# Transposed blocks by way of HBM, the norm of rows 0 at five boundaries too, and out-projections that end with three units per quarter

## The chip, the core and the metric

The kernel runs on one core of a Trainium2 chip. The metric is device time in microseconds (us) of one execution; less is better. TensorE (PE) multiplies, VectorE (DVE) and ScalarE (ACT) do element work, GpSimd (POOL) does a little of it, SyncE (SP) issues most DMAs. Each engine works through its own fixed list of instructions in order, and a semaphore wait at the head of a list stops all that stands behind it.

## What is computed

A decoder trunk of two layers over 256 rows of 1024 columns. Each layer is a half-step SwiGLU FFN, a mixer (A in layer 0: chunked spatial gating; B in layer 1: causal pooling), and a second half-step FFN, each behind an RMSNorm, and a last RMSNorm:

```
for i in range(DEPTH):
    x = x + 0.5 * swiglu(rmsnorm(x, ffn_norm[i, 0]), ffn_w_in[i, 0], ffn_w_out[i, 0])
    h = rmsnorm(x, mix_norm[i])
    x = x + (chunked_sgu if i % 2 == 0 else pool_mixer)(h, ...)
    x = x + 0.5 * swiglu(rmsnorm(x, ffn_norm[i, 1]), ffn_w_in[i, 1], ffn_w_out[i, 1])
return rmsnorm(x, final_norm)
```

Six sublayers follow each other, so there are five boundaries at which the residual `x` is normed and turned for the next in-projection.

## The kernel before

The 256 rows are two tiles, rows 0 (t = 0) and rows 1 (t = 1), of 128 partitions. Every f32 product is made of three fp32r matmuls (`mm3`, L126 to L131): high by high, high by low, low by high, so each operand is split into a rounded high part (`hh`, `gh`, `whi`) by ACT and the rest (`hl`, `gl`, `wlo`) by DVE.

Weights come in halves of 128x1024 (512 KB). `fetch` issues one on SP's queue into one of four `raw` buffers; `split_piece` makes `whi` on ACT and, two ticks later, `wlo` on DVE, which then issues the next `fetch`. There are eight pairs of split halves (`W_BUFS`): a half can only be split when the half eight before it has been released by PE's last use of it.

The order of all engines' lists is written by the program itself: each `mm3` is one tick, `later(n, fn)` has `fn` recorded n ticks further on, and `pump` records a split every two or three ticks when a buffer is released. So a work item's place in a list is set by ticks (one tick is three matmuls of PE), not by when its data is ready.

`proj_in` computes 512 columns (a chunk) at a time: for rows 0 all eight k, then for rows 1 all eight, with four weight halves; the next four halves serve the next chunk. `proj_out` keeps four accumulators (two rows tiles by two halves of the columns, the quarters). The first `n - LAG` units (256 values of k, two weight halves each) go through all four quarters unit by unit; the last `LAG` units go quarter by quarter, so that each quarter ends on its own: rows 0 left, rows 0 right, rows 1 left, rows 1 right. Behind each quarter stands its residual add (`x<-mm,x`, L361) and `half(t, h)` (L295): multiply by the gain (`xs`, L298), four ticks later four PE transposes of 128x128 into PSUM (`tp<-ident,xs`, L304), then ACT's `hh` and DVE's `hl` from PSUM (L238, L239), then the squares for the norm (L248). The reciprocal root is applied later, behind the in-projection.

The FFN's gated values and mixer A's outputs are needed with k on partitions too. They are turned by DVE in 32x32 squares (`gq<-g`, L374), and 16 DMAs for each pair of chunks move the squares between partition groups from `gq` to `ge`, SBUF to SBUF, half of them issued by SP and half by POOL (L387). `trip` ticks later ACT and DVE split `ge` into `gh` and `gl` (L398, L399): 32 ticks in the FFNs, 24 in mixer A. Mixer B makes its `gh` and `gl` per group from PSUM (L625, L630).

Of the kernel before, what the change touches and what calls it, by code (L numbers as in the profile page):

```python
# [11 lines left out]
F32 = mybir.dt.float32  # L12
F32R = mybir.dt.float32r
AF = mybir.ActivationFunctionType
ALU = mybir.AluOpType

P = 128
# [8 lines left out]
HEADS = 8  # L26
# [4 lines left out]
NCH = FF // 256  # L31
# [4 lines left out]

RAW_BUFS = 4
W_BUFS = 8
LAG = 2
PACE = 3  # L40
LOW = 2
HOP = 3
GATE = 10
T2K = 8
BATCH = 2


@with_exitstack
def trunk_kernel(
# [22 lines left out]
    nc = tc.nc  # L72
    V, A, G, PE = nc.vector, nc.scalar, nc.gpsimd, nc.tensor
# [4 lines left out]
    hp = ctx.enter_context(tc.tile_pool(name="hp", bufs=1))  # L78
    gp = ctx.enter_context(tc.tile_pool(name="gp", bufs=24))
    sq = ctx.enter_context(tc.tile_pool(name="sq", bufs=2))  # L80
    tmp = ctx.enter_context(tc.tile_pool(name="tmp", bufs=2))
    tiny = ctx.enter_context(tc.tile_pool(name="tiny", bufs=4))
    pm = ctx.enter_context(tc.tile_pool(name="pm", bufs=6, space=bass.MemoryType.PSUM))
# [8 lines left out]
    def f32(ap):  # L92
        return ap.bitcast(F32)

    def t2k(name):
        return tmp.tile([P, 512], F32, name=name, tag="t2k", bufs=T2K)

    def g_tile(name, cols=None):
        return gp.tile(cols or [P, 2, S], F32R, name=name, tag="g2k")
# [6 lines left out]
    def later(n, fn):  # L106
        pending.append([n, fn])
# [28 lines left out]
    for i in range(DEPTH):  # L136
        j = i // 2
# [93 lines left out]
    def scaled(a, b, name):  # L231

        o = tiny.tile([P, 1], F32, name=name, tag="scaled", bufs=12)
        V.tensor_scalar(o, a, b, None, op0=ALU.mult)
        return o

    def split(ps, hi, lo, gap=1):
        A.copy(hi, ps)  # L238
        low = lambda: V.tensor_tensor(lo, ps, f32(hi), op=ALU.subtract)  # L239
        if gap:  # L240
            later(gap, low)
        else:
            low()

    def square(t, c):
        sq = t2k("sq")
        a = tiny.tile([P, 1], F32, name="ssq", bufs=6)
        A.activation(sq[:, :c.stop - c.start], x[t][:, c], AF.Square, scale=1.0 / 32.0, accum_out=a)  # L248
        return a

    def rstd(t, parts):
        ms = tiny.tile([P, 1], F32, name="ms")
        V.tensor_scalar(ms, parts[0], parts[1], EPS, op0=ALU.add, op1=ALU.add)  # L253
        return rsqrt(ms, f"rstd{t}")

    def norm_T(gain, factors):


        hT = [[None, None, None, []] for _ in range(NT)]
        ssq = {0: [], 1: []}  # L260

        def tiles(t, h):
            if h == 0:
                for e, n in enumerate(("hh", "hl")):
                    hT[t][e] = hp.tile([P, KD * P], F32R, name=f"{n}{t}", tag=f"{n}{t}")
            return hT[t][:2]

        def stat(t, h):
            ssq[t].append(square(t, slice(h * 512, (h + 1) * 512)))
            if h == 1:  # L270
                later(1, lambda: rows(t))

        def rows(t):
            r = hT[t][2] = rstd(t, ssq[t])
            later(1, lambda: hT[t][3].extend(scaled(r, r if f is None else f, f"r{t}") for f in factors))

        def first(t, h):

            ps = pt.tile([P, 4, P], F32, name="tp", tag="tp")
            for e in range(4):  # L280
                k = 4 * h + e
                PE.transpose(ps[:, e, :], x[t][:, k * P:(k + 1) * P], ident)  # L282
            c = slice(h * 512, (h + 1) * 512)
            hh, hl = tiles(t, h)
            xs = t2k("xs")
            g = gcol[:, 4 * h:4 * h + 4].unsqueeze(2).to_broadcast([P, 4, P])
            V.tensor_tensor(xs.rearrange("p (k t) -> p k t", k=4), ps, g, op=ALU.mult)

            def fin():
                A.copy(hh[:, c], xs)  # L290
                V.tensor_tensor(hl[:, c], xs, f32(hh[:, c]), op=ALU.subtract)  # L291

            return fin

        def half(t, h):  # L295
            c = slice(h * 512, (h + 1) * 512)
            xs = t2k("xs")
            V.tensor_tensor(xs, x[t][:, c], gain[0][:, c], op=ALU.mult)  # L298
            state["hush"] = 4

            def turn():
                ps = pt.tile([P, 512], F32, name="tp", tag="tp")
                for k in range(4):
                    PE.transpose(ps[:, k * P:(k + 1) * P], xs[:, k * P:(k + 1) * P], ident)  # L304
                hh, hl = tiles(t, h)
                split(ps, hh[:, c], hl[:, c])
                later(2, lambda: stat(t, h))

            later(4, turn)

        return half, first, stat, hT

    def proj_in(chunks, hT, use, first=False):
# [20 lines left out]
    def proj_out(n, lhs, scale, half, tail=False):  # L334
# [7 lines left out]
        def part(u, t, h):  # L342
            c = segs[t][h]
            for j in range(2):
                k = 2 * u + j
                if len(w) <= k:
                    w.append(take())
                hi, lo = w[k]
                mm3(acc[t][h], *lhs(k, t), hi[:, c], lo[:, c], k == 0, k == 2 * n - 1)
                if t == NT - 1 and c.stop == D:  # L350
                    release()

        for u in range(n - LAG):
            for t in range(NT):
                for h in range(len(segs[t])):
                    part(u, t, h)
        for t in range(NT):
            for h, c in enumerate(segs[t]):
                for u in range(n - LAG, n):
                    part(u, t, h)  # L360
                V.scalar_tensor_tensor(x[t][:, c], acc[t][h], scale(t), x[t][:, c], op0=ALU.mult, op1=ALU.add)  # L361
                half(t, h)

    def turned(n, out, trip, closing=False):

        squares = {}

        def put(c, t, src):  # L370
            b, m = c // BATCH, min(BATCH, n - c // BATCH * BATCH)
            if b not in squares:
                squares[b] = sq.tile([P, 4, m, 2, NT, 32], F32, name="gq", tag="gq")
            V.transpose(  # L374
                squares[b][:, :, c % BATCH, :, t, :].rearrange("p q k i -> p k q i"),
                src.rearrange("p (k q j) -> p k q j", k=2, q=4),
            )
            if t == NT - 1 and c % BATCH == m - 1:
                later(2, lambda: move(b, m))

        def move(b, m):

            e = sq.tile([P, 4, m, 2, NT, 32], F32, name="ge", tag="ge")
            to = "p c k t i -> p (c k t i)"
            for q in range(4):
                for a in range(4):
                    (G if a % 2 else nc.sync).dma_start(e[32 * q:32 * q + 32, a].rearrange(to), squares[b][32 * a:32 * a + 32, q].rearrange(to))  # L387
            if closing and b == (n - 1) // BATCH:
                G.drain()
            for c in range(m):  # L390
                later(trip + 3 * c, lambda c=c: take_in(b * BATCH + c, e[:, :, c]))

        def take_in(c, e):
            hi, lo = g_tile("gh"), g_tile("gl")
            src = e.rearrange("p a k t i -> p a (k t) i")
            to = "p k (t a i) -> p a (k t) i"
            h, l = (x.rearrange(to, t=NT, a=4) for x in (hi, lo))
            A.copy(h, src)  # L398
            later(1, lambda: V.tensor_tensor(l, src, f32(h), op=ALU.subtract))  # L399
            out[c] = hi, lo  # L400

        return put

    def ffn(i, hT, half, first=False, tail=False):

        gT, rh, r2 = {}, {}, {}
        put = turned(NCH, gT, 32, closing=tail)

        def use(c, t, ps):
            if c == 0:  # L410
                rh[t], r2[t] = hT[t][3]
            th = tmp.tile([P, 256], F32, name="th", tag="c1k", bufs=2)
            A.activation(th, ps[:, 0:256], AF.Tanh, scale=rh[t])  # L413

            def mul():
                s = tmp.tile([P, 256], F32, name="s", tag="c1k", bufs=2)
                V.scalar_tensor_tensor(s, th, 1.0, ps[:, 0:256], op0=ALU.add, op1=ALU.mult)  # L417
                g = tmp.tile([P, 256], F32, name="g", tag="g1k", bufs=4)
                V.scalar_tensor_tensor(g, s, r2[t], ps[:, 256:512], op0=ALU.mult, op1=ALU.mult)  # L419
                later(1, lambda: put(c, t, g))  # L420

            later(1, mul)

        proj_in(NCH, hT, use, first)

        def lhs(k, t):
            hi, lo = gT[k // 2]
            return hi[:, k % 2, t * P:(t + 1) * P], lo[:, k % 2, t * P:(t + 1) * P]

        proj_out(NCH, lhs, lambda t: 0.25, half, tail)  # L430
# [13 lines left out]
    def mixer_a(j, hT, half, prep, next_gain):  # L444
        vn_g, wm, bs = prep
        vn_g.append(load_gain(a_v_norm[j, D:2 * D]))
        r, vs, ssq, yT, ws, k_sq, k_th, half_r, rv = {}, {}, {0: [], 1: []}, {}, {}, {}, {}, {}, {}
# [83 lines left out]
                    later(GATE + t_, lambda t_=t_: gate(q, t_))  # L531

        us = {}
        put = turned(HEADS, yT, 24)

        def gate(q, t):
            vh, vl = vs[q, t]
# [138 lines left out]
    with tc.manual_schedule(engines={E.PE, E.Activation, E.DVE, E.Pool, E.SP}):  # L676
# [28 lines left out]
        _, first, stat, hT = norm_T(None, FFN_R)  # L705
# [106 lines left out]
```

## Time and profile before

| what | value |
| --- | --- |
| median of 3 runs | 937.83 us (937.55 to 939.37) |
| the profiled execution, own time | 938.44 us |
| its span in the trace | 936.7 us |
| PE busy | 927.7 us (99%), granted clock 0.998 |
| DVE, ACT, POOL busy | 649.2, 478.1, 135.3 us |
| DMA | 195.63 MB, mean 209 GB/s |

The span is what the instructions cover; the execution's own time is 1.7 us longer. Busy time of PE includes matmuls that overlap (one takes 390 ns and the next starts some 227 ns later), so what counts on PE is the distance from start to start and any gap in it.

### The profile page before, as it was taken

The numbers are of one execution on the slowest core, as the hardware profiler recorded it, in microseconds if no ns is written. First come the engines' busy times: TensorE is split into PE (matmuls) and PEld (weight loads), VectorE is DVE, ScalarE is ACT, GpSimd is POOL, SyncE is SP. The second block draws the span as 40 slices with busy tenths as digits, with TensorE's granted clock in tenths as the row PEclk, the third lists the DMA queues.
The fourth block names the chain that finished last, engine by engine and source line by source line (L and its number), as shares of the span: only waits on it lengthen the run. The fifth ranks groups of instructions, "written<-read, shape, count | busy, mean of one in ns | idle before, by whom it ended". The sixth has DMA issues, their size and how long they took to land.

```text
span 936.7 us, 12478 instructions
## 1 busy us (share of the span) xinstructions
PE 927.7 (99%) x4238; PEld 769.4 (82%) x4238; DVE 649.2 (69%) x880; ACT 478.1 (51%) x641; POOL 135.3 (14%) x256
## 2 busy tenths in 40 slices
PE   9999999999999999999999999999999999999997
PEld 6888888888888888888888888888888888888886
DVE  6877774578898686777645867775467787777642
ACT  6555554368765364554533545545355464445431
POOL 0111130013233001112200032111000002221100
PEclk9999999999999999999999999999999999999999
DMA  6777877556477647776754677777555566677731
GB/s 239 234 246 253 240 260 234 177 193 198 149 241 238 212 164 222 223 241 212 241 193 135 225 218 223 230 242 254 185 173 183 180 205 222 211 246 212 232 123 45
DMA packets 68960, 195.63 MB, mean 209 GB/s; under 512 B 13216, under 2 KB 20896, under 8 KB 68896
## 3 DMA queue, kind: packets, MB, share of 16 engines
q1 hardware_dynamic: 61152, 187.22, 62.0%
q0 software_dynamic: 7168, 6.83, 2.6%
q10 hardware_dynamic: 576, 0.79, 0.2%
q8 instruction: 33, 0.54, 0.2%
q14 instruction: 31, 0.25, 0.1%
HBM read 180.11 MB, written 1.05 MB: 193 GB/s over the span
## 4 chain that ended last, share of the span: by engine, by line
PE 98%; DVE 1%; DMA 0%; ACT 0%; issue 0%; POOLq 0%; POOL 0%; ACTq 0%
PE mm L128 32%; PE mm L129 32%; PE mm L130 32%; PE tp L304 1%; DMA x<-in_x 0%; PE tp L129 0%; PE tp L130 0%; PE tp L128 0%; PE mm L697 0%; DVE x L361 0%; PE tp L282 0%; ACT sq L248 0%; PE tp L603 0%; PE tp L604 0%; PE tp L606 0%
## 5 line engine op out<-in xcount | busy, mean ns | idle before, releaser
L180 DVE TENSOR_TENSOR wlo<-raw,whi 128x1024 fp32r<-128x1024 f32 (+1 forms) x334 | 401.6, 1215 | 157.0 <-ACT whi L175 148.2
L175 ACT CAST whi<-raw 128x1024 fp32r<-128x1024 f32 (+1 forms) x334 | 343.4, 1042 | 221.0 <-PE mm L130 150.9
L128 PE MATMUL mm<-whi,hh 128*128 128x512 f32 x864 | 338.3, 392 | 0.1
L129 PE MATMUL mm<-wlo,hh 128*128 128x512 f32 x864 | 336.4, 389 | 0.0
L130 PE MATMUL mm<-whi,hl 128*128 128x512 f32 x864 | 336.4, 389 | 0.0
L130 PEld LDWEIGHTS mm<-whi,hl 128*128 128x128 f32 x864 | 162.3, 188 | 34.4 <-DVE hl L291 0.4
L128 PEld LDWEIGHTS mm<-whi,hh 128*128 128x128 f32 x864 | 162.4, 188 | 33.9 <-ACT hh L290 0.5
L129 PEld LDWEIGHTS mm<-wlo,hh 128*128 128x128 f32 x864 | 162.4, 188 | 32.9
L128 PE MATMUL mm<-whi,gh 128*128 128x512 f32 (+1 forms) x470 | 179.4, 382 | 0.0
L130 PE MATMUL mm<-whi,gl 128*128 128x512 f32 (+1 forms) x470 | 178.4, 379 | 0.0
L129 PE MATMUL mm<-wlo,gh 128*128 128x512 f32 (+1 forms) x470 | 178.3, 379 | 0.0
L387 POOL DMA_DIRECT2D ge<-gq x224 | 110.3, 500 | 400.1 <-ACT gh L398 245.7
L413 ACT ACTIVATE th<-mm,r 128x256 f32<-128x256 f32 x88 | 41.8, 475 | 129.6 <-PE mm L130 128.3
L130 PEld LDWEIGHTS mm<-whi,gl 128*128 128x128 f32 x470 | 88.4, 188 | 16.9
L129 PEld LDWEIGHTS mm<-wlo,gh 128*128 128x128 f32 x470 | 88.5, 188 | 16.2
L128 PEld LDWEIGHTS mm<-whi,gh 128*128 128x128 f32 x470 | 88.4, 188 | 16.2
L417 DVE SCALAR_TENSOR_TENSOR s<-th,mm 128x256 f32<-128x256 f32 x88 | 37.1, 421 | 61.1 <-ACT th L413 61.0
L228 POOL TENSOR_TENSOR rstd<-ms,neg_half 128x1 f32<-128x1 f32 x14 | 7.8, 554 | 344.2 <-DVE ms L253 344.2
L419 DVE SCALAR_TENSOR_TENSOR g<-s,r,mm 128x256 f32<-128x256 f32 x88 | 42.3, 481 | 3.1
L374 DVE STREAM_TRANSPOSE gq<-g 128x256 f32<-128x256 f32 x88 | 39.2, 445 | 2.9
L238 ACT CAST hh<-tp 128x512 fp32r<-128x512 f32 x20 | 11.8, 589 | 47.6 <-PE tp L304 47.6
L399 DVE TENSOR_TENSOR gl<-ge,gh 128x512 fp32r<-128x512 f32 x52 | 35.3, 684 | 0.0
(86 smaller groups left out, 337.7 us busy)
## 6 DMA issues: line engine op xcount, KB each, us to landing
raw<-in_ffn_w_in SPq DMA_DIRECT2D x174, 512.0 KB, 4.6
raw<-in_ffn_w_out SPq DMA_DIRECT2D x88, 512.0 KB, 5.0
raw<-in_a_w_in SPq DMA_DIRECT2D x32, 512.0 KB, 4.1
raw<-in_a_w_out SPq DMA_DIRECT2D x16, 512.0 KB, 5.0
ge<-gq POOLq DMA_DIRECT2D x192, 32.0 KB, 4.4
ge<-gq SPq DMA_DIRECT2D x192, 32.0 KB, 4.1
raw<-in_b_w_in SPq DMA_DIRECT2D x8, 512.0 KB, 3.8
raw<-in_b_w_out SPq DMA_DIRECT2D x8, 512.0 KB, 4.7
```

Of the source, the lines that this page charges most:

```text
L128: PE.matmul(acc, lhsT=ah, rhs=bh, start=start, stop=False)
L129: PE.matmul(acc, lhsT=ah, rhs=bl, start=False, stop=False)
L130: PE.matmul(acc, lhsT=al, rhs=bh, start=False, stop=stop)
L175: A.copy(hi[:, c], raw[:, c])
L180: V.tensor_tensor(lo[:, c], raw[:, c], f32(hi[:, c]), op=ALU.subtract)
L238: A.copy(hi, ps)
L374: V.transpose(squares[b][:, :, c % BATCH, :, t, :].rearrange("p q k i -> p k q i"), src.rearrange("p (k q j) -> p k q j", k=2, q=4),)
L387: (G if a % 2 else nc.sync).dma_start(e[32 * q:32 * q + 32, a].rearrange(to), squares[b][32 * a:32 * a + 32, q].rearrange(to))
L399: later(1, lambda: V.tensor_tensor(l, src, f32(h), op=ALU.subtract))
L413: A.activation(th, ps[:, 0:256], AF.Tanh, scale=rh[t])
L417: V.scalar_tensor_tensor(s, th, 1.0, ps[:, 0:256], op0=ALU.add, op1=ALU.mult)
L419: V.scalar_tensor_tensor(g, s, r2[t], ps[:, 256:512], op0=ALU.mult, op1=ALU.mult)
```

## The change

1. A new DRAM pool `hbm` (two buffers). `quadrants` writes all squares of a batch from `gq` to HBM in one DMA, and `TURN` = 4 ticks later issues four DMAs that read them back into the four partition groups of `ge`. All five are on SP's queue. `turned` uses it in place of the 16 DMAs; POOL issues no DMA any more, and the drain of POOL in the last FFN is gone.
2. At the boundaries `half` for rows 0 no longer uses PE: DVE turns `xs` in 32x32 squares at once, `quadrants` moves them by way of HBM, and `WAY` = 11 ticks later ACT and DVE split `ge` into `hh` and `hl`. Rows 1 keep the PE transposes.
3. `LAG` goes from 2 to 3: the last three units are done quarter by quarter, 18 matmuls in each quarter where there were 12.
4. Mixer A's `trip` goes from 24 to 17 ticks.

```diff
-LAG = 2
+LAG = 3
+TURN = 4
+WAY = 11
+    hbm = ctx.enter_context(tc.tile_pool(name="hbm", bufs=2, space=bass.MemoryType.DRAM))
...
-            later(4, turn)
+            def across():
+                z = sq.tile([P, 4, 4, 32], F32, name="gq", tag="gq")
+                V.transpose(z.rearrange("p q k i -> p k q i"), xs.rearrange("p (k q j) -> p k q j", k=4, q=4))
+                e = sq.tile([P, 4, 4, 32], F32, name="ge", tag="ge")
+                quadrants(z.rearrange("p q k i -> p q (k i)"), [e[32 * q:32 * q + 32].rearrange("p a k i -> p a (k i)") for q in range(4)], P)
+                later(WAY, lambda: take_in(e))
+            def take_in(e):
+                hh, hl = (o[:, c].rearrange("p (k a i) -> p a k i", k=4, a=4) for o in tiles(t, h))
+                A.copy(hh, e)
+                later(1, lambda: V.tensor_tensor(hl, e, f32(hh), op=ALU.subtract))
+                later(2, lambda: stat(t, h))
+            if t == 0:
+                across()
+            else:
+                later(4, turn)
...
+    def quadrants(squares, to, n):
+        d = hbm.tile([P, 4, n], F32, name="dq", tag="dq")
+        nc.sync.dma_start(d, squares)
+        src = d.rearrange("(a j) q n -> q j a n", a=4)
+        def back():
+            for q in range(4):
+                nc.sync.dma_start(to[q], src[q])
+        later(TURN, back)
...
-            for q in range(4):
-                for a in range(4):
-                    (G if a % 2 else nc.sync).dma_start(e[32 * q:32 * q + 32, a].rearrange(to), squares[b][32 * a:32 * a + 32, q].rearrange(to))
-            if closing and b == (n - 1) // BATCH:
-                G.drain()
+            quadrants(squares[b].rearrange("p q c k t i -> p q (c k t i)"), [e[32 * q:32 * q + 32].rearrange("p a c k t i -> p a (c k t i)") for q in range(4)], m * 128)
...
-        put = turned(HEADS, yT, 24)
+        put = turned(HEADS, yT, 17)
```

In the rows below the numbers behind the names are buffers; line numbers of the changed kernel are its own (L178 there is L175 before, L183 is L180, L241 is L238, L251 is L248, L381 is L361, L301 is L298, L307 is L304, L131 to L133 are L128 to L130).

First place: ACT's list at the first boundary, from the FFN to mixer A. Before:

```order
L175 CAST whi_1698<-raw_1636 128x1024
L175 CAST whi_1713<-raw_1651 128x1024
L238 CAST hh0_1742<-tp_1737 128x512
L248 ACTIVATE sq_1755,ssq_1756<-x0_85 128x512
L238 CAST hh0_1742<-tp_1764 128x512
L248 ACTIVATE sq_1780,ssq_1781<-x0_85 128x512
L238 CAST hh1_1798<-tp_1793 128x512
L175 CAST whi_1807<-raw_1672 128x1024
L248 ACTIVATE sq_1824,ssq_1825<-x1_86 128x512
L238 CAST hh1_1798<-tp_1836 128x512
L175 CAST whi_1842<-raw_1687 128x1024
```

And in the changed kernel:

```order
L178 CAST whi_1604<-raw_1542 128x1024
L178 CAST whi_1619<-raw_1557 128x1024
L322 CAST hh0_1691<-ge_1639 128x4x4x32
L251 ACTIVATE sq_1704,ssq_1705<-x0_87 128x512
L241 CAST hh1_1721<-tp_1716 128x512
L178 CAST whi_1724<-raw_1578 128x1024
L322 CAST hh0_1691<-ge_1669 128x4x4x32
L251 ACTIVATE sq_1735,ssq_1736<-x1_88 128x512
L251 ACTIVATE sq_1752,ssq_1753<-x0_87 128x512
L241 CAST hh1_1721<-tp_1774 128x512
L178 CAST whi_1780<-raw_1593 128x1024
```

Before, the four halves of the next in-projection's first chunk (1662, 1677, 1698, 1713) are split ahead of the boundary and 1807 is already of the second chunk; in the changed kernel only two (1604, 1619) are, and the third (1724) and fourth (1780) stand behind the two casts of `hh1`, which wait for the transposes of rows 1. DVE's list there, in the changed kernel:

```order
L381 SCALAR_TENSOR_TENSOR x0_87<-mm_1289,x0_87 128x512
L301 TENSOR_TENSOR xs_1665<-x0_87,gain_938 128x512
L315 STREAM_TRANSPOSE gq_1667<-xs_1665 128x4x4x32
L323 TENSOR_TENSOR hl0_1692<-ge_1639,hh0_1691 128x4x4x32
L381 SCALAR_TENSOR_TENSOR x1_88<-mm_1290,x1_88 128x512
L301 TENSOR_TENSOR xs_1699<-x1_88,gain_938 128x512
L242 TENSOR_TENSOR hl1_1722<-tp_1716,hh1_1721 128x512
L183 TENSOR_TENSOR wlo_1725<-raw_1578,whi_1724 128x1024
L323 TENSOR_TENSOR hl0_1692<-ge_1669,hh0_1691 128x4x4x32
L381 SCALAR_TENSOR_TENSOR x1_88<-mm_1291,x1_88 128x512
L301 TENSOR_TENSOR xs_1743<-x1_88,gain_938 128x512
```

The residual add and the gain of the last quarter (`x1<-mm_1291`, `xs_1743`) now stand behind `wlo_1725` and both `hl0`; before, they stood behind the `hl0` of the second transposes and some operations of one column.

Second place: PE's list at the same boundary in the changed kernel, from the second turn of rows 1 on (`mm_1747` is rows 0 of the first chunk):

```order
L307 MATMUL tp_1774<-ident_89,xs_1743 128x128 x4
L131 MATMUL mm_1747<-whi_1724,hh0_1691 128x512
L132 MATMUL mm_1747<-wlo_1725,hh0_1691 128x512
L133 MATMUL mm_1747<-whi_1724,hl0_1692 128x512
L131 MATMUL mm_1747<-whi_1724,hh0_1691 128x512
L132 MATMUL mm_1747<-wlo_1725,hh0_1691 128x512
L133 MATMUL mm_1747<-whi_1724,hl0_1692 128x512
L131 MATMUL mm_1747<-whi_1780,hh0_1691 128x512
L132 MATMUL mm_1747<-wlo_1781,hh0_1691 128x512
```

Eighteen matmuls stand between the two turns of rows 1, as before; between the second turn and the first use of the fourth half (`whi_1780`, `wlo_1781`) stand six. The other four boundaries have the same rows in the same places.

Third place: PE's list in mixer B of the changed kernel, behind the last group's matmuls (`tp_6565`, split into `gh_6578`, `gl_6579`):

```order
L133 MATMUL tp_6565<-qh_6510,wlo_6241 128x256
L131 MATMUL mm_6461<-whi_6469,gh_6550 128x512
L132 MATMUL mm_6461<-wlo_6470,gh_6550 128x512
L133 MATMUL mm_6461<-whi_6469,gl_6551 128x512
L131 MATMUL mm_6461<-whi_6513,gh_6550 128x512
L132 MATMUL mm_6461<-wlo_6514,gh_6550 128x512
L133 MATMUL mm_6461<-whi_6513,gl_6551 128x512
L131 MATMUL mm_6461<-whi_6531,gh_6578 128x512
L132 MATMUL mm_6461<-wlo_6532,gh_6578 128x512
L133 MATMUL mm_6461<-whi_6531,gl_6579 128x512
L131 MATMUL mm_6461<-whi_6582,gh_6578 128x512
L132 MATMUL mm_6461<-wlo_6583,gh_6578 128x512
```

Before, 18 matmuls of the second unit stood between the last group and the first quarter's two last units; now the last group's own values are used six matmuls behind it, and `whi_6582` and `wlo_6583` stand behind its `gh` on ACT and its `gl` on DVE.

## Rows read from the trace of the kernel before

**Rows 1.** The page: busy time by engine, and the last chain by engine.

```profile
PE 927.7 (99%) x4238; PEld 769.4 (82%) x4238; DVE 649.2 (69%) x880; ACT 478.1 (51%) x641; POOL 135.3 (14%) x256
...
PE 98%; DVE 1%; DMA 0%; ACT 0%; issue 0%; POOLq 0%; POOL 0%; ACTq 0%
```

**Rows 2.** Waits of PE: us in total, times, longest.

```profile
PE mm L697 <- DVE warm L692: 1.3, 1, 1.3
PE tp L282 <- DMA x<-in_x: 1.0, 2, 0.8
```

**Rows 3.** Timeline of PE, first boundary, second turn of rows 1: start, us.

```profile
195.23 0.60 PE L304 MATMUL tp<-ident,xs 128*128 128x128 f32 x4
195.58 0.48 PE L128 MATMUL mm<-whi,hh 128*128 128x512 f32 x1
195.89 0.40 PE L129 MATMUL mm<-wlo,hh 128*128 128x512 f32 x1
196.13 0.40 PE L130 MATMUL mm<-whi,hl 128*128 128x512 f32 x1
...
197.05 0.40 PE L128 MATMUL mm<-whi,hh 128*128 128x512 f32 x1
197.29 0.39 PE L129 MATMUL mm<-wlo,hh 128*128 128x512 f32 x1
```

**Rows 4.** Timeline of ACT at the first boundary.

```profile
195.86 0.59 ACT L238 CAST hh<-tp 128x512 fp32r<-128x512 f32 x1 [1.02 <-PE tp L304]
196.34 1.05 ACT L175 CAST whi<-raw 128x1024 fp32r<-128x1024 f32 x1
```

**Rows 5.** Timeline of DVE at the first boundary.

```profile
183.12 0.69 DVE L361 SCALAR_TENSOR_TENSOR x<-mm,x 128x512 f32<-128x512 f32 x1 [1.08 <-PE mm L130]
183.84 0.69 DVE L298 TENSOR_TENSOR xs<-x,gain 128x512 f32<-128x512 f32 x1
...
185.85 0.69 DVE L361 SCALAR_TENSOR_TENSOR x<-mm,x 128x512 f32<-128x512 f32 x1 [0.17 <-PE mm L130]
...
190.37 0.68 DVE L239 TENSOR_TENSOR hl<-tp,hh 128x512 fp32r<-128x512 f32 x1
190.97 0.20 DVE L253 TENSOR_SCALAR ms<-ssq 128x1 f32<-128x1 f32 x1
...
197.43 1.22 DVE L180 TENSOR_TENSOR wlo<-raw,whi 128x1024 fp32r<-128x1024 f32 x1 [0.26 <-ACT whi L175]
...
199.63 1.22 DVE L180 TENSOR_TENSOR wlo<-raw,whi 128x1024 fp32r<-128x1024 f32 x1
200.77 0.68 DVE L455 SCALAR_TENSOR_TENSOR ga<-ga,mm 128x512 f32<-128x512 f32 x1
```

**Rows 6.** DMA issues: operation, count, KB each, median us to landing.

```profile
raw<-in_a_w_in SPq DMA_DIRECT2D x32, 512.0 KB, 4.1
...
ge<-gq SPq DMA_DIRECT2D x192, 32.0 KB, 4.1
...
out<-o SPq DMA_DIRECT2D x2, 256.0 KB, 2.0
```

**Rows 7.** Lines L374 and L387: ns min/median/max; landing us min/median/max.

```profile
L374 DVE STREAM_TRANSPOSE gq<-g x88: 436/446/449, 23.4 to 870.6; 128x256 f32<-128x256 f32 x88
...
L387 SPq DMA_DIRECT2D ge<-gq x224: 507/589/1693, 39.2 to 877.5; - x112
...
DMA to landing us min/median/max: 1.7/4.3/6.4
```

**Rows 8.** Timeline of mixer B behind its last group: PE, ACT, DVE.

```profile
732.35 0.40 PE L128 MATMUL mm<-whi,gh 128*128 128x512 f32 x1
...
732.55 0.84 ACT L625 ACTIVATE gh<-tp,sc 128x256 fp32r<-128x256 f32 x2 [1.98 <-PE tp L130]
...
733.43 0.88 DVE L630 SCALAR_TENSOR_TENSOR gl<-tp,sc,gh 128x256 fp32r<-128x256 f32 x2 [1.94 <-ACT gh L625]
734.37 1.23 DVE L180 TENSOR_TENSOR wlo<-raw,whi 128x1024 fp32r<-128x1024 f32 x1
```

**Rows 9.** PE's warm-up, and windows: us, busy by engine, granted clock.

```profile
1.26 2.31 PE L697 MATMUL mm<-warm 128*128 128x512 bf16 x5 [1.26 <-DVE warm L692]
...
930.00:937.00 7.00, 0.00 (x0) 0.00 (x0) 1.47 (x6) 1.51 (x6) 0.55 (x1) 0.65 0.20 75
```

More of the change, by code (lines that the diff above doesn't have):

```diff
@@ L362, in proj_out, with turned @@
                 half(t, h)
-    def turned(n, out, trip, closing=False):
+    def quadrants(squares, to, n):
[6 more added lines that the diff above has]
+        later(TURN, back)
+    def turned(n, out, trip):
         squares = {}
@@ L383, in move @@
             e = sq.tile([P, 4, m, 2, NT, 32], F32, name="ge", tag="ge")
-            to = "p c k t i -> p (c k t i)"
-            for q in range(4):
-                for a in range(4):
-                    (G if a % 2 else nc.sync).dma_start(e[32 * q:32 * q + 32, a].rearrange(to), squares[b][32 * a:32 * a + 32, q].rearrange(to))
-            if closing and b == (n - 1) // BATCH:
-                G.drain()
+            quadrants(squares[b].rearrange("p q c k t i -> p q (c k t i)"), [e[32 * q:32 * q + 32].rearrange("p a c k t i -> p a (c k t i)") for q in range(4)], m * 128)
             for c in range(m):
@@ L406, in ffn @@
         gT, rh, r2 = {}, {}, {}
-        put = turned(NCH, gT, 32, closing=tail)
+        put = turned(NCH, gT, 32)
         def use(c, t, ps):
```

## The prediction

> **What bounds the kernel now.** The page comes first: PE is busy for 99% of the span, and the chain that ended last runs through PE for 98% [rows 1]. The list of PE's waits then tells whether that is work or waiting: it has two entries, both at the start, 2.3 us in all [rows 2]. So past its first microseconds PE never waits for anyone, and the time is the sum of the distances between its matmuls. Only two things can move it: fewer instructions on PE, or a wait where there is none. For a wait the views of one boundary matter, engine by engine [rows 3 to 5], since every engine's order is fixed ahead.
>
> I count time at a boundary from the first matmul behind the first quarter (rows 0 left). The residual add of a quarter starts 0.2 behind that point. Two adds in a row without a turn between them stand 2.73 apart (183.12 and 185.85, [rows 5]) for 12 matmuls, so a matmul is 0.227 and a new quarter of 18 is 4.09.
>
> **What is removed.** Forty PE transposes, ten groups of four. A group starts at 195.23 and the second matmul behind it at 195.89: 0.66 where two starts are otherwise 0.23 apart, so a group costs 0.43 to 0.45; with 0.44, ten groups are **4.4 us less** [rows 3]. Nothing else leaves PE.
>
> **What the longer quarters do to the weights (LAG).** There are eight pairs of split halves. With two units held for four quarters four are held and four free, which are the first chunk's four halves. With three units six are held, so halves 3 and 4 of the next chunk can only be split in and behind the last quarter. The order shows where: on ACT each stands behind a cast of `hh1`, which waits for a PE transpose of rows 1.
>
> *The fourth half.* Before, the same chain can be read behind the second turn: transposes at 195.23, cast 195.86, `whi` 196.34, `wlo` 197.43 to 198.65, that is 3.42 from start to end [rows 3 to 5]. Nobody waited for that half, since it belonged to the second chunk. Now PE wants it behind six matmuls: the row that takes `wlo` is the eighth behind the turn, which stood at 197.29, 2.06 behind the start. 3.42 + 0.05 for the semaphore - 2.06 = **1.4 us per boundary, 7.0 for five**.
>
> *The third half.* On DVE its `wlo` and then an `hl0` stand ahead of the last quarter's add and gain, which the second turn needs. From the start of the first turn: cast 0.63 later, `whi` 0.48 later, `wlo` 1.09 later, then 1.14 to the next operation (199.63 to 200.77), `hl0` 0.60 (190.37 to 190.97), add 0.72 (183.12 to 183.84), gain 0.69, semaphore 0.05: 5.40 [rows 3 to 5]. PE reaches the second turn after 0.44 + 18 x 0.227 = 4.53. It waits **0.87 per boundary, 4.4 for five**. What is queued behind it on PE is the whole in-projection. The fourth half starts from that turn, so the two waits add.
>
> **What the way through HBM does.** For rows 0 left: add at 0.2, gain 0.72 later, DVE transposes 0.72 later. A transpose of 128x256 takes 0.446 [rows 7], so one of 512 columns between that and 0.89; I take 0.7. SP issues the write at 2.4. The nearest row for a write to HBM of the same 256 KB is the output at the end, on an idle queue: 2.0 [rows 6]. At 4.4 the four reads are issued, at some 0.6 each [rows 7], the last at 6.2. Their landing no row shows. The nearest by shape is the move of squares, 1.7 at best and 4.3 in the median, with weight loads in flight [rows 7]. The order has no weight load between the write and the reads here, so I take 2.0, like the output: 8.2 to 8.3. Then cast, `hl0`, add, gain of rows 1 left (0.65 + 0.65 + 0.72 + 0.69 and semaphores, 2.76): its turn can start at 11.0, where PE arrives at 2 x 4.09 + 12 x 0.227 = 10.9. So 0.1 at the low end, zero with a landing of 1.7, and 2.4 with 4.3. The last weight load was issued 3 us before the write and takes 4.1 in the median [rows 6], so the write may land some tenths later: I take **0.4 for each of four boundaries, 1.6**. For rows 0 right the same steps start at 4.3, but SP is busy with the first reads until 6.7: landing at 12.3 to 12.5, where the third half's chain asks for it at 13.5. That one is covered by 1 us. At the fifth boundary (mixer B to FFN) the order has a weight load between the first write and its reads and one ahead of the second write; at up to 4.1 each I add 0.4 more to the first and 0.9 to the second, **1.7 there**. Together 3.3 (bounds 0 and 13).
>
> The Trainium skill, "DMA: Bandwidth & Descriptors", section "Anatomy of one DMA", puts a fixed cost of about 2.0 us on each DMA, most of it the confirmed write at the target, heaviest at HBM. By it (an estimate from that page) each trip pays this twice in a row; the output's 2.0 agrees, the squares' 4.3 is more than that page gives for 32 KB within SBUF, and with 4.3 for the reads the total below would be 9 us higher.
>
> **Mixer B.** The last group's matmuls end as 732.35 starts. `gh` is done 1.04 behind that point, `gl` 1.96, `whi` of the last half 1.98, its `wlo` at 735.60, 3.25 [rows 8]. Now PE wants `gl` at 8 x 0.23 = 1.85 and that `wlo` at 10 x 0.23 + 0.15 of waiting, 2.5: waits of 0.15 and 0.8, **0.95 once**.
>
> **At nothing.** The pairs of chunks: 2.0 to 4.1 for the write, 2.4 for four issues, 2.0 to 4.3 for the last read, 6 to 11, against 32 ticks of 0.68 (21.8) in the FFNs. In mixer A 17 ticks are 11.6, and the last pair is wanted about 6 ticks (4.1) later still; two weight loads stand between its write and reads, which would use up that cover but not exceed it. Five DMAs on SP replace eight on SP and eight on POOL; SP now stops until the write lands, and the weight loads behind it come up to 4 later; eight split halves are 8 x 2.72 of PE's time. POOL loses its issues and the drain, and nobody waits for POOL there. The end is unchanged: the last add hangs on PE's last matmul either way.
>
> **Sum.** -4.4 + 7.0 + 4.4 + 3.3 + 0.95 = +11.2. On the profiled execution's own 938.44 that is 949.7; it stands 0.6 above the median of the runs, so I forecast **949.1 us**, 1.2% slower.
>
> **The rivals.**
> - *The transposes saved are all that counts: 933.4 us.* This ends on the other side. It needs both halves' splits to be done in time: the two waits decide, and the change breaks even where they fall from 2.27 to 0.88 per boundary (with nothing for the trip). For it: no chain of ACT and DVE ever held PE up before [rows 2], and steps between two rows may hold idle time that shrinks. Against it: in the chains read above ACT and DVE start each step as soon as its input is there or the step ahead of it lets them, and the halves' places in the lists are fixed.
> - *Only one of the two waits appears.* If `hl0` and the add of the last quarter get ahead of the third half's `wlo` in effect, 4.4 goes and 944.7 remains; with the trip at its lower bound of 0 too, 941.4.
> - *The reads land like the squares, 4.3 us.* Then the first turn waits 2.4 at four boundaries and about 3.7 at the fifth: 13.3 in place of 3.3, 959.1 us. For it: the median of 224 moves [rows 7]; against: no weight load is issued into that gap.
> - *The clock falls in the new waits.* The granted clock is at its full level of 2.4 GHz throughout and falls only where PE has been idle at the end [rows 9]. The warm-up matmuls took 2.31 for five, 0.46 each, twice the 0.227. If 24 matmuls behind each boundary ran like that, 24 x 0.23 x 5 = 28 us more, 977. Pauses of 0.8 at the start [rows 2] changed nothing. [...]
>
> **How the numbers follow.** The forecast's case has 0.61, one wait only 0.12, late reads 0.13, the clock 0.03, the bare saving 0.07, and 0.04 for a balance of waits and saving. A measurement of this kernel tells 0.2% from no change, here 1.9 us. Faster is the bare saving and a little of the balance, 0.08; within 0.2% 0.03; slower 0.89. The range of 941 to 957 holds the forecast with its trip between 0 and about 11, and the case of one wait; what it leaves out is the bare saving, the latest reads and the clock.
>
> **What would show each step.** In the changed kernel's list of PE's waits: about 1.4 us five times at a high-by-low matmul, released by DVE's `wlo`; about 0.9 five times at the transposes, released by DVE's `xs`; a few tenths at the first turn, released the same way, with ACT's `hh` waiting for `ge`; two short waits in mixer B. The write `dq<-gq` at the boundaries should land in 2 to 3 us and the reads in about 2. PE should have 40 transposes left. I am wrong if PE's waits stay under 4 us in all (then the saving wins), if ACT's wait for `ge` exceeds 3 us at each boundary, or if the granted clock shows its lower level in the middle of the span.

## The result, and the profile after

The changed kernel takes **950.33 us** (median of 4 runs, 949.76 to 952.73); the kernel before, beside it, 937.90 (4 runs). The ratio is 1.0134, with a 95% interval of 1.0122 to 1.0146: 1.3% slower. The profiled execution took 950.13 us, with a span of 948.3, 11.6 more than the span before.

The page after, busy time and last chain by engine, answers to [rows 1].

```profile
PE 927.6 (98%) x4198; PEld 764.3 (81%) x4198; DVE 655.3 (69%) x890; ACT 475.3 (50%) x641; POOL 25.6 (3%) x32
...
PE 82%; DVE 8%; DMA 5%; ACT 2%; issue 2%; SPq 0%; POOL 0%; ACTq 0%; POOLq 0%; DVEq 0%
```

PE has 40 instructions fewer and hardly less busy time: a matmul counts as busy for its modelled 0.39, while in a row the next starts after 0.227, so some 0.16 of every gap is counted as busy, and that hides much of what the transposes saved. The chain says what happened: it no longer stays on PE, but leaves it for DVE, DMA and ACT, which hold 15% of the span together. The list of PE's waits after names the places (it answers to [rows 2]):

```profile
PE tp L307 <- DVE xs L301: 6.0, 6, 1.6
PE mm L132 <- DVE wlo L183: 4.9, 7, 0.8
PE mm L723 <- DVE warm L718: 1.3, 1, 1.3
PE mm L131 <- ACT whi L178: 1.2, 5, 0.2
PE tp L285 <- DMA x<-in_x: 1.1, 2, 0.7
```

Two of the five are the old ones of the start. The other three are new, 12.1 us in 18 waits. A wait in this list begins only at that modelled end, so the gaps below are measured from start to start, less the normal distance. The timeline of PE at the first boundary, second turn of rows 1 (it answers to [rows 3]):

```profile
193.97 0.39 PE L133 MATMUL mm<-whi,hl 128*128 128x512 f32 x1
195.06 0.66 PE L307 MATMUL tp<-ident,xs 128*128 128x128 f32 x4 [0.71 <-DVE xs L301]
...
196.71 0.39 PE L133 MATMUL mm<-whi,hl 128*128 128x512 f32 x1
197.34 0.51 PE L131 MATMUL mm<-whi,hh 128*128 128x512 f32 x1 [0.24 <-ACT whi L178]
198.60 0.51 PE L132 MATMUL mm<-wlo,hh 128*128 128x512 f32 x1 [0.76 <-DVE wlo L183]
```

Before the turn 1.09 from start to start, so 0.86 lost; then 0.63 and 1.26, so 0.40 and 1.03 lost on the fourth half. Between the two turns of rows 1 stand 18 matmuls here; in the kernel before there were 12 (turns at 192.04 and 195.23), and not 18 as the section on the change has it. The lists of ACT and DVE there show what the turn and that half waited for (they answer to [rows 4, 5]). ACT:

```profile
190.77 1.05 ACT L178 CAST whi<-raw 128x1024 fp32r<-128x1024 f32 x1
...
195.76 0.59 ACT L241 CAST hh<-tp 128x512 fp32r<-128x512 f32 x1 [2.18 <-PE tp L307]
196.24 1.05 ACT L178 CAST whi<-raw 128x1024 fp32r<-128x1024 f32 x1
```

DVE:

```profile
191.86 1.22 DVE L183 TENSOR_TENSOR wlo<-raw,whi 128x1024 fp32r<-128x1024 f32 x1 [0.26 <-ACT whi L178]
193.00 0.68 DVE L323 TENSOR_TENSOR hl<-ge,hh 128x512 fp32r<-128x512 f32 x1
193.60 0.68 DVE L381 SCALAR_TENSOR_TENSOR x<-mm,x 128x512 f32<-128x512 f32 x1
194.32 0.69 DVE L301 TENSOR_TENSOR xs<-x,gain 128x512 f32<-128x512 f32 x1
...
197.32 1.23 DVE L183 TENSOR_TENSOR wlo<-raw,whi 128x1024 fp32r<-128x1024 f32 x1 [0.25 <-ACT whi L178]
```

From 190.77 on there is no pause in the chain `whi`, `wlo`, `hl0`, add, gain, turn. ACT's cast of the fourth half (196.24) stands behind a cast that needs the turn (195.76), and ACT idles 2.18 in front of that cast. SP's queue at the first and at the second boundary shows the way through HBM:

```profile
181.16 0.33 SPq L387 DMA_DIRECT2D dq<-gq  x1
183.18 1.75 SPq L392 DMA_DIRECT2D ge<-dq  x4
...
318.21 1.47 SPq L165 DMA_DIRECT2D raw<-in_ffn_w_in  x2
321.48 0.33 SPq L387 DMA_DIRECT2D dq<-gq  x1
325.19 1.75 SPq L392 DMA_DIRECT2D ge<-dq  x4
```

The reads are issued when the write has landed: 2.0 later at the first boundary; 3.7 later at the second, where two weight loads of 512 KB were issued just ahead, 3.3 and 2.1 before the write. At the first the last load was issued 3.5 before it. Medians of all writes and reads of these sizes, ten of the boundaries and four of the FFNs' last chunks (DMA issues, to [rows 6]):

```profile
dq<-gq SPq DMA_DIRECT2D x14, 256.0 KB, 2.2
ge<-dq SPq DMA_DIRECT2D x56, 64.0 KB, 2.0
```

All gaps that are new, boundary by boundary:

| place | gaps, us | sum | forecast |
| --- | --- | --- | --- |
| second turn of rows 1 (third half) | 0.86, 0.94, 0.84, 0.89, 1.60 | 5.13 | 4.4, and 0.9 of the trip at the fifth |
| fourth half, `whi` and `wlo` | 1.43 five times | 7.15 | 7.0 |
| first turn of rows 1 (trip) | 0, 1.80, 0, 0, 0.26 | 2.06 | 2.4 |
| mixer B, out-projection | 0.99 | 0.99 | 0.95 |
| mixer B, in-projection | 0.48 | 0.48 | none |
| transposes that went | | -4.4 | -4.4 |

That is 15.8 less 4.4, 11.4 of the 11.6 by which the span grew.

### The profile page after: what moved, and what is told of

Read it like the earlier page. It is cut to its first block, busy times and chain, and to the rows that moved or that the text cites. A ratio compares the mean times of both kernels' runs of the same rounds, so it can differ in the third digit from the quotient of the medians.

```text
span 948.3 us, 11685 instructions
## 1 busy us (share of the span) xinstructions
PE 927.6 (98%) x4198; PEld 764.3 (81%) x4198; DVE 655.3 (69%) x890; ACT 475.3 (50%) x641; POOL 25.6 (3%) x32
## 4 chain that ended last, share of the span: by engine, by line
PE 82%; DVE 8%; DMA 5%; ACT 2%; issue 2%; SPq 0%; POOL 0%; ACTq 0%; POOLq 0%; DVEq 0%
PE mm L132 27%; PE mm L133 27%; PE mm L131 26%; DVE wlo L183 3%; DMA dq<-gq 2%; ACT whi L178 2%; DMA raw<-in_a_w_out 1%; DMA ge<-dq 1%; DVE xs L301 1%; DVE x L381 1%; DVE y L574 1%; SPq L392 0%; DMA x<-in_x 0%; DVE hl L323 0%; DVE u L489 0%
## 5 line engine op out<-in xcount | busy, mean ns | idle before, releaser
L183 DVE TENSOR_TENSOR wlo<-raw,whi 128x1024 fp32r<-128x1024 f32 (+1 forms) x334 | 399.9, 1213 | 141.5 <-ACT whi L178 136.6
L178 ACT CAST whi<-raw 128x1024 fp32r<-128x1024 f32 (+1 forms) x334 | 341.4, 1039 | 204.9 <-PE mm L133 130.3
L131 PE MATMUL mm<-whi,hh 128*128 128x512 f32 x864 | 338.3, 392 | 1.2 <-ACT whi L178 1.2
L133 PE MATMUL mm<-whi,hl 128*128 128x512 f32 x864 | 336.3, 389 | 0.0
L131 PEld LDWEIGHTS mm<-whi,hh 128*128 128x128 f32 x864 | 162.4, 188 | 36.8 <-ACT whi L178 3.3
L133 PEld LDWEIGHTS mm<-whi,hl 128*128 128x128 f32 x864 | 162.2, 188 | 34.2 <-DVE hl L294 0.4
L131 PE MATMUL mm<-whi,gh 128*128 128x512 f32 (+1 forms) x470 | 178.9, 381 | 0.0
L133 PE MATMUL mm<-whi,gl 128*128 128x512 f32 (+1 forms) x470 | 178.2, 379 | 0.0
L133 PEld LDWEIGHTS mm<-whi,gl 128*128 128x128 f32 x470 | 88.4, 188 | 16.7
L131 PEld LDWEIGHTS mm<-whi,gh 128*128 128x128 f32 x470 | 88.4, 188 | 16.5 <-ACT whi L178 0.2
L424 ACT CAST gh<-ge 128x512 fp32r<-128x512 f32 x52 | 31.8, 618 | 4.9 <-DMA ge<-dq 4.9
L322 ACT CAST hh<-ge 128x512 fp32r<-128x512 f32 x10 | 6.2, 620 | 51.9 <-DMA ge<-dq 51.9
L381 DVE SCALAR_TENSOR_TENSOR x<-mm,x 128x512 f32<-128x512 f32 (+1 forms) x21 | 13.9, 663 | 22.1 <-PE mm L133 22.1
```

Of the source, the lines that this page charges most:

```text
L131: PE.matmul(acc, lhsT=ah, rhs=bh, start=start, stop=False)
L133: PE.matmul(acc, lhsT=al, rhs=bh, start=False, stop=stop)
L178: A.copy(hi[:, c], raw[:, c])
L183: V.tensor_tensor(lo[:, c], raw[:, c], f32(hi[:, c]), op=ALU.subtract)
```

## The experiments

The theory (**held halves**): three units per quarter hold six of eight pairs, so the third and fourth half of the next chunk are split behind the casts of the turns; that is what makes PE wait. The rival (**trip**): the norm's way through HBM makes the boundary late, and the waits on weights only show it.

**The parts, one at a time.** First the kernel before with only the longer quarters and mixer A's 17 ticks; nothing goes through HBM.

```diff
-LAG = 2
+LAG = 3
-        put = turned(HEADS, yT, 24)
+        put = turned(HEADS, yT, 17)
```

> The kernel before with LAG = 3 and mixer A's trip of 17 ticks, and nothing else: all turns on PE, squares moved within SBUF. Theory W (the weight halves that six held buffers push behind the casts of hh1 hold PE up): the fourth half costs 1.4 us at each of five boundaries as in the changed kernel, the third half only about 0.3 each, since no hl0 stands ahead of the last quarter's add here (5.40 - 0.60 against 4.53), and mixer B 1.0: 937.9 + 7.0 + 1.4 + 1.0 = 947.3 us. Rival T (the trip through HBM, on which ACT waits 52 us in the changed kernel, is what costs): there is no trip, so about 938, plus at most 1 for mixer B.

949.59 us (949.50 to 949.88), ratio 1.0123 [1.0108, 1.0138]. Without any trip, and without the transposes' saving, it is 11.5 slower, 2.3 more than the theory had. Its gaps: 1.43 at each of the five fourth halves, 0.33 to 0.39 at each second turn of rows 1, 1.00 and 0.47 in mixer B, 0.24 at the second turn of rows 0 at the fifth boundary, 10.6 of the 11.1 by which the span (947.8) is longer. The list of PE's waits of this kernel:

```profile
PE mm L129 <- DVE wlo L180: 4.9, 7, 0.8
...
PE mm L128 <- ACT whi L175: 1.2, 5, 0.2
PE tp L304 <- DVE xs L298: 1.0, 5, 0.2
```

The waits on `wlo` and `whi` are the same, to a tenth, as in the changed kernel (4.9 and 1.2). At the second turn of rows 1 the gap is only 0.33 to 0.39; `hl0` (0.60) does not stand in DVE's list there. So the changed kernel is made up of this one's 11.5, some 0.5 for `hl0` at each of five boundaries and 2.8 of late trips, less 4.4 for the transposes. That gives 12.4, and its median lies 12.4 above that of the kernel before.

Next the reverse: the pairs of chunks through HBM, and nothing else.

```diff
-LAG = 3
+LAG = 2
-            if t == 0:
+            if False:
-        put = turned(HEADS, yT, 17)
+        put = turned(HEADS, yT, 24)
```

> The changed kernel with LAG = 2, mixer A's trip of 24 and PE turns for rows 0 as before: only the pairs of chunks go through HBM. Both theories: covered by 32 and 24 ticks, 937.9 within 1 us, PE without waits. If SP's stops for the write starve the weight loads, PE waits for ACT's split in the FFNs and it is 2 us or more slower.

938.02 us, ratio 1.0001 [0.9991, 1.0010], and no wait of PE behind the start. The pairs cost nothing, as forecast, and the eight DMAs per pair that POOL no longer issues bring nothing.

Then the changed kernel without the move at the boundaries; this leaves out the exchange between partition groups, so `hh` and `hl` of rows 0 hold unmoved squares.

```diff
-                e = sq.tile([P, 4, 4, 32], F32, name="ge", tag="ge")
-                quadrants(z.rearrange("p q k i -> p q (k i)"), [e[32 * q:32 * q + 32].rearrange("p a k i -> p a (k i)") for q in range(4)], P)
-                later(WAY, lambda: take_in(e))
+                later(WAY, lambda: take_in(z))
```

> The changed kernel without the move at the boundaries: hh and hl of rows 0 are split from gq, the squares as DVE turned them, so rows 0 of the next in-projection get their squares in the wrong partition groups; all lists keep their order. Theory W: the waits for the third and fourth halves stay (0.87 and 1.4 at each boundary), and only the late first turns go (1.8 at the second boundary, 0.3 and 0.7 at the fifth): 950.3 - 2.8 = 947.5. Rival T: with the trip gone the saving of 4.4 shows, about 934 to 936.

946.95 us, ratio 1.0092 [1.0076, 1.0109]. The gaps at the first turn are gone; those at the second (0.84 to 0.90, five times) and at the fourth half (1.43, five times) stay. The trip is worth 950.33 - 946.95 = 3.4 us of the whole, against 3.3 in the sum. As the main cause the rival falls: some 9 us of the slowdown stay without it.

The fourth part is the trip with two units per quarter.

```diff
-LAG = 3
+LAG = 2
-        put = turned(HEADS, yT, 17)
+        put = turned(HEADS, yT, 24)
```

> The change with two units per quarter (mixer A's own squares at 24 ticks again), so that four halves of the next chunk are split ahead, while the norm of rows 0 still goes through HBM at the five boundaries. Theory 'the held halves alone cost' says that the trip as such is free and the 40 transposes' 4.4 us come off: 933.5. Theory 'the trip is free only behind long quarters' says that a quarter of 12 matmuls (2.7 us) is too short: rows 0 left is wanted about 1.0 too early at each boundary and rows 0 right about 0.5 more, 1.6 x 5 - 4.4 = 3.6 slower, 941.5. Theory 'late reads' (landing at 4.3) says 950 or more.

944.37 us, ratio 1.0068 [1.0054, 1.0082]. With short quarters the trip is not free, as the second of the three theories has it, but that theory's size was too small: eight waits of 0.25 to 1.6 on `hh0` in this one line of PE's list, 6.1 in all, where the estimate had 1.0 and 0.5 at each boundary. From start to start these waits, with the three slower starts behind each turn (0.34 to 0.39 apart), come to some 11.4; less 4.4 that is 7.0, where the medians grew by 6.4. SP's queue shows what the estimate lacked: at every boundary a weight load is issued between the first write and its reads, and these land in 2.6 to 3.8 in place of 2.0.

```profile
PE mm L131 <- ACT hh L322: 6.1, 8, 1.6
```

So the longer quarters give the trip its time, and as the change makes them they cost more than they give: 950.33 against 944.37.

**When the halves are split.** `half` sets `hush` to 4 (L302): for four ticks behind a quarter, until its turn, no split is recorded. With three units held, halves 3 and 4 come free in the last quarter, and both fall into such a pause, so each lands behind a cast that needs the turn. The edit takes the pause away, in the changed kernel and then in the kernel of longer quarters alone.

```diff
-            state["hush"] = 4
+            state["hush"] = 0
```

> The changed kernel with the pause of four ticks behind half (hush) taken out, so that the third half's split is recorded ahead of the first cast of hh1 and the fourth's ahead of the second. Theory W: both waits go at all five boundaries (about 0.9 and 1.4 each, 11.5 in all), the late first turns and mixer B's 1.0 stay: 950.3 - 11.5 = 938.8. Rival T: the trip is as long as before, about 950.

> The kernel before with three units per quarter and the splits not held back behind a norm (hush 0); no transposed block goes through HBM. Theory 'the third and fourth half are split too late' says that both waits go and mixer B's 1.0 and 0.5 stay: 938.1 + 1.5 = 939.6. A rival in which the three units cost by themselves (more matmuls behind the turn that wait for a cast) says that it stays with the kernel of three units alone, 949.6.

939.82 us (ratio 1.0018 [0.9998, 1.0038]) and 939.32 (1.0011 [1.0002, 1.0020]). In both, the waits on both halves are gone at all five boundaries. In the second only mixer B's 0.99 is left behind the start, so all that the longer quarters cost at the boundaries was the order of splits and casts. The first spread over 936.4 to 945.8; its profiled run, 939.8, lost most at the fifth boundary, and what the slowest runs lost is not shown. PE's timeline there:

```profile
743.75 0.39 PE L133 MATMUL mm<-whi,gl 128*128 128x512 f32 x1
747.03 0.66 PE L307 MATMUL tp<-ident,xs 128*128 128x128 f32 x4 [2.89 <-DVE xs L301]
747.44 0.64 PE L131 MATMUL mm<-whi,gh 128*128 128x512 f32 x1
747.88 0.63 PE L132 MATMUL mm<-wlo,gh 128*128 128x512 f32 x1
```

and its windows (us, PE busy, granted clock, DMA share, GB/s):

```profile
744.00:747.00 3.00, 0.14 (x1) 1.00 0.17 51
747.00:751.00 4.00, 3.97 (x13) 0.57 0.50 158
751.00:755.00 4.00, 4.00 (x21) 1.00 0.26 76
```

The turn waited 3.05, and then eight matmuls ran 0.43 apart in place of 0.227, at a granted clock of about half, the 1.2 GHz level. That is the forecast's clock rival, at one place, at a cost of some 1.6 us. In SP's queue at that place:

```profile
735.46 0.33 SPq L387 DMA_DIRECT2D dq<-gq  x1
736.57 1.46 SPq L165 DMA_DIRECT2D raw<-in_ffn_w_in  x2
738.08 1.85 SPq L392 DMA_DIRECT2D ge<-dq  x4
```

Two weight loads are issued between the write and its reads, and the reads, which `hh0`, `hl0`, the add and the turn follow, land in 4.7 to 5.6. In the changed kernel one load stood there, and they landed in 2.4 to 3.0. No kernel here moved these loads alone.

**Where late reads are waited for.** DVE's `hl0` of rows 0 left, which needs ACT's cast of the reads, stands in DVE's list ahead of the add of rows 1 left (`WAY` = 11), so a late read stops the turn although nobody wants `hl0` yet. First a kernel with early splits that avoids only the worst place: mixer B with two units, and PE turns for rows 0 at the fifth boundary.

```diff
-    def norm_T(gain, factors):
+    def norm_T(gain, factors, trip=True):
...
-            if t == 0:
+            if t == 0 and trip:
...
-        proj_out(4, lhs, lambda t: 1.0, half)
+        proj_out(4, lhs, lambda t: 1.0, half, lag=2)
...
-            half, _, _, nxt = norm_T(g, FFN_R)
+            half, _, _, nxt = norm_T(g, FFN_R, i % 2 == 0)
```

> The change with hush 0, and at the fifth boundary (mixer B to FFN) two units and PE turns for rows 0 as before; the other four boundaries go through HBM. Theory 'the wait of 3 us and the low clock behind it are what is left': from the 939.8 of the profiled early split go 3.05 of waiting, some 1.8 of slow matmuls and mixer B's 0.99, and 0.88 of transposes comes back: 934.8, 0.35% faster than the kernel before, with a spread no wider than that kernel's. Rival 'the early split moved something else, and the fifth boundary is only where it shows': 937 to 940 with the same wide spread.

937.33 us, ratio 0.9992 [0.9981, 1.0003], and a spread of 935.3 to 939.9: the time is the rival's (937 to 940) and not the theory's 934.8, though the spread is half of the early split's. The fifth boundary is clean, but the first turn of rows 1 waits elsewhere, 2.21 at the second boundary and 1.55 at the fourth. SP at the second (write to reads 3.6; a load just ahead, one more 1.1 before it), then DVE:

```profile
316.73 0.33 SPq L165 DMA_DIRECT2D raw<-in_ffn_w_in  x1
318.86 0.33 SPq L387 DMA_DIRECT2D dq<-gq  x1
322.42 1.76 SPq L392 DMA_DIRECT2D ge<-dq  x4
```

```profile
326.49 0.69 DVE L323 TENSOR_TENSOR hl<-ge,hh 128x512 fp32r<-128x512 f32 x1 [4.46 <-ACT hh L322]
327.10 0.75 DVE L381 SCALAR_TENSOR_TENSOR x<-mm,r,x 128x512 f32<-128x512 f32 x1
```

Then the same kernel, and the changed kernel with early splits, and the changed kernel by itself, each with `hl0` three ticks later:

```diff
-WAY = 11
+WAY = 14
```

> The mended kernel (hush 0; fifth boundary with two units and PE turns) with WAY 14 in place of 11: rows 0 left are taken in behind the add and gain of rows 1 left, so that a late read no longer stands ahead of that turn. Theory 'the waits of 2.2 and 1.6 us at the first turn are reads that landed late, queued ahead of the add on DVE' says that both go: 937.9 - 3.8 = 934.1, 0.4% faster than the kernel before, with a narrower spread. Rival 'the late reads are then waited for where PE wants hh0': 936 to 938, with waits at a matmul that reads hh0 or hl0.

> The early split (hush 0) with WAY 14, all five boundaries through HBM, three units in mixer B too. Theory 'the wait of 3 us at the fifth boundary is a read that landed late ahead of the add, and the low clock behind it follows from the wait' says that 0.5, 3.05 and the 1.8 of slow matmuls go: 939.8 - 5.3 = 934.5, and the clock keeps its full level. Rival 'the read is late for hh0 too': 936 to 940.

> The change with WAY 14 alone. On DVE hl0 now stands behind the add of the last quarter, but on ACT a square of 0.53 gets between the cast of hh1 and whi behind both turns. Theory 'the two waits are the sums of what stands in those lists' says: second turn 0.87 - 0.60 + 0.53 = 0.8, fourth half 1.43 + 0.53 = 1.96, first turn none: 950.3 - 2.8 - 0.3 + 2.65 = 949.9. Rival 'the trip is what counts': without the waits of the first turn and with a freer last quarter 943 to 947.

The first: **934.61 us** (933.63 to 936.91), ratio 0.9964 [0.9952, 0.9977]. This is faster than both kernels, by 0.4% and 1.7%. In its profiled run, the fastest of six, PE's list of waits is back to the start alone:

```profile
PE mm L723 <- DVE warm L718: 1.3, 1, 1.3
PE tp L285 <- DMA x<-in_x: 1.0, 2, 0.8
```

At the second boundary its reads are nearly as late as before the edit. SP and DVE there:

```profile
318.46 0.33 SPq L387 DMA_DIRECT2D dq<-gq  x1
321.88 1.75 SPq L392 DMA_DIRECT2D ge<-dq  x4
```

```profile
323.95 0.75 DVE L381 SCALAR_TENSOR_TENSOR x<-mm,r,x 128x512 f32<-128x512 f32 x1 [1.85 <-PE mm L133]
324.74 0.69 DVE L301 TENSOR_TENSOR xs<-x,gain 128x512 f32<-128x512 f32 x1
325.95 0.69 DVE L323 TENSOR_TENSOR hl<-ge,hh 128x512 fp32r<-128x512 f32 x1 [0.52 <-ACT hh L322]
```

The write still takes 3.4, but the add and the gain now stand ahead of `hl0`. With a landing nearly as late, the place in the list made the difference between 2.2 and nothing. At the fourth boundary the write landed earlier (2.46, where it had been 3.95), so the 1.55 there is no test of the edit.

The second: 935.77 us, ratio 0.9969 [0.9957, 0.9981], 1.3 above the forecast of 934.5. The wait of 3.05 became 0.34 at the turn and 0.78 at a matmul that wants `hl0`, so both theories hold a part; the clock kept its full level. The reads at the fifth boundary were again late (4.4 to 5.3, two loads between the write and them).

The third: 953.12 us, ratio 1.0151 [1.0138, 1.0164]: slower than the changed kernel, and 3.2 above its own forecast. The sizes were as expected: no gap at the first turn, 0.84 to 0.94 at the second (expected 0.8), 2.04 at the fourth half (1.96), where a square of 0.62 now stands between the cast and `whi`: the gap grew by 0.61. What was not expected is the clock. The windows at the second and at the third boundary (us, busy by engine, granted clock, DMA share, GB/s):

```profile
336.00:339.80 3.80, 2.19 (x9) 1.27 (x8) 2.63 (x7) 3.80 (x8) 0.76 (x2) 1.00 0.15 56
339.80:343.20 3.40, 3.40 (x9) 2.60 (x8) 2.58 (x6) 2.07 (x3) 1.37 (x1) 0.51 0.79 263
...
522.00:525.00 3.00, 1.41 (x6) 0.68 (x5) 2.25 (x7) 3.00 (x7) 0.79 (x2) 1.00 0.01 3
525.00:529.00 4.00, 4.00 (x19) 3.31 (x18) 3.52 (x8) 2.92 (x4) 1.34 (x1) 1.00 0.75 250
```

Behind nearly the same three gaps (0.84 to 0.94, 1.0, 1.03) some eight matmuls ran 0.43 apart at the second and at the fourth boundary, 1.5 to 1.6 us each, and none at the other three. Together that is 3.1 of the missing 3.2.

## Why the prediction was right

The forecast was 949.1 and the result is 950.33. The waits came at the places and in the sizes that the sum has, with the exceptions below.

- **The saving, 4.4.** PE has 40 instructions fewer, all of them transposes. In the kernel of 934.61, which waits for nothing behind the start, four boundaries' saving shows: 32 transposes, 3.5 by the forecast's 0.44 per group, and 3.8 measured between the medians.
- **Fourth half, 1.4 at each boundary.** Measured 1.43 five times; shown by the kernel of longer quarters alone, where it stands without any trip, and by the early split, where it goes.
- **Third half, 0.87.** Measured 0.84 to 0.94 at four boundaries. Its parts are shown too: without `hl0` in the list 0.33 to 0.39 is left.
- **The trip, 3.3.** The sum was right, 2.8 by gaps and 3.4 by leaving it out, but by luck: its spread over the boundaries was not. I put 0.4 on each of four boundaries; three had nothing and the second had 1.80. At the first the forecast's times were right up to the reads (write at 2.4, reads at 4.4 behind the first matmul of the second quarter), but the four reads take 0.43 each to issue and not 0.6, and `hh` began at 7.8 in place of 8.2. At the second the write took 3.7 behind two weight loads, a thing that I named ("may land some tenths later") and sized too small by a factor of four. So I carried too much at four boundaries and too little at the one where two loads had just been issued, and the errors cancelled. At the fifth it was 0.26 and some 0.7, where I had 0.8 and 0.9.
- **The landing of 2.0.** The changed kernel's own medians are 2.2 for the write and 2.0 for the reads. The Trainium skill's "DMA: Bandwidth & Descriptors", section "Anatomy of one DMA", which describes DMAs that GpSimd issues, puts the fixed cost at about 2.0, with the time of the bytes on top; these DMAs are issued by SP, and their 2.0 holds the moving of 256 KB too, so the fixed part here is less than that. The 3.7 behind two loads is beyond it.
- **A sign that misled.** I wrote that I am wrong if ACT's wait for `ge` exceeds 3 us at each boundary. It did: ACT was idle 8.4 to 10.9 in front of the first such cast at all five. It was a bad sign. The cast comes next in ACT's list behind the last split, and ACT stands idle from there on, long before PE needs `hh0`; at three of the five boundaries PE lost nothing to the trip. From the list of ACT's waits in the changed kernel:

```profile
ACT hh L322 <- DMA ge<-dq: 51.9, 6, 10.9
```

- **Mixer B, 0.95.** Measured 0.99, all of it at `wlo` of the last half; the wait of 0.15 on `gl` ahead of it did not appear by itself. A further 0.48, in mixer B's own in-projection, I had missed: `wlo` is late there too, and the kernel of longer quarters alone shows the same 0.47.
- **The pairs at nothing.** Shown: 1.0001.
- **The clock, 0.03.** It kept its full level in the changed kernel, with a longest gap of 1.80. Two variants show that the rival was near. One argument against it was none: around the pauses of 0.8 at the start the warm-up matmuls ran 0.43 apart, at the lower level already, so these pauses could not show a fall.

Three slips in the working changed nothing. Reads that land in 4.3 would add 10 us (13.3 in place of 3.3) and not 9. With mixer B's 0.95 the change breaks even at 0.69 per boundary and not at 0.88. And the clock was not at its full level throughout: the first matmuls ran 0.43 apart, until about 10 us.

My range was 941 to 957, and what I gave to "only one of the two waits" was more than it deserved: both come from the same pause in splitting, and they came and went together in every kernel here that kept or dropped that pause.

## What to carry to other kernels

Longer quarters and an early start of a transfer both hold something back (here six of eight split buffers), and the cost shows where the next consumer's first operands are made, not where the edit is. Where an order is written ahead, ask of each late item what it stands in front of: three ticks in one list turned a late read's 2.2 us into nothing, with a write that still took 3.4 where it had taken 3.6. Undo the parts one by one before giving up a change: of this one the transposes saved were worth 0.4%, and the places of the splits and of `hl0` in the lists had hidden it.

## What the runs showed of the hardware

PE's clock fell behind pauses in the middle of a busy span. Behind a gap of 3.05 (the early split) eight matmuls ran 0.43 apart, with 0.57 granted over 4 us. This fits the warning in the Trainium skill's "TensorE: Matmul & The Clock Gate", section "Why this matters for your kernels", about idle gaps. A gap of 2.21 (the kernel with 937.33) left the full level, 1.00 over the next 4 us. What I had not expected is that several gaps of about 1 us, close together, were followed by the same at two of five like places, granted 0.51 and 0.52 over some 3.4 us, and not at the other three. In the changed kernel gaps of 0.84 to 1.60, 0.40 and 1.03 never did. What decides between like places I did not find out; it stays open.

A write of 256 KB to HBM landed in 2.0 us at the first boundary, where the last load of 512 KB had been issued 3.5 ahead and landed 0.8 behind the write's issue. At the second it landed in 3.4 to 3.7 in four kernels, with loads issued 3.3 and 2.1 ahead; each time that is some 0.65 behind the landing of the later load (2.75 to 3.05). Reads of 64 KB took 1.8 to 2.3 with no load between the write and them, 2.4 to 3.8 with one (the trip with two units, and the fifth boundary of the changed kernel), and 4.4 to 5.6 with two (the early splits at the fifth boundary). A write of 3.95 at the fourth boundary of the kernel with 937.33 had no load nearer than 3.5 ahead, and its cause is open. Whether the queue or the shared DMA engines make that difference was not tried.
